# A hybrid encoder layer on one core: gate rows spread by broadcast loads in place of selector matmuls

## The chip, the cores and the metric

The kernel runs on one core of a Trainium2 chip. The metric is the device time of one launch in microseconds. Five engines work side by side, each through its own instructions in order: TensorE (PE, with PEld for the loading of its stationary operand), VectorE (DVE), ScalarE (ACT), GpSimd (POOL) and SyncE (SP), which here only issues DMA transfers. They wait for each other by semaphores.

## The reference

One pre-norm layer on 256 tokens of width 2048, in float32: RMSNorm, one wide input projection, an mLSTM branch and an RG-LRU branch, both in both directions, a sigmoid-gated merge, an output projection, a residual and a last RMSNorm. What the change touches is the weights of the mLSTM branch, with 4 heads and 2 directions:

```python
d_log = jnp.where(lower, bc[..., :, None] - bc[..., None, :] + ic[..., None, :], -jnp.inf)
inter_log = bc + m_st[..., None]
m_row = jnp.maximum(inter_log, jnp.max(d_log, axis=-1))
w_intra = jnp.exp(d_log - m_row[..., None])
scores = jnp.einsum('bhjk,bhsk->bhjs', qc, kc) * w_intra
...
h = num / jnp.maximum(jnp.abs(den), jnp.exp(-m_row))[..., None]
```

Here `bc` is the running sum of the log of the forget gate and `ic` the input gate. The weight of key position s for query position j is an exponential of something that depends on j alone (the row maximum, one number for each partition) plus something that depends on s alone (`ic - bc`, one row of 256 numbers for each head and direction, eight rows in all). The kernel puts the queries on the partitions, so a row over s has to be present in every partition.

## The kernel before, in words

**Products.** Weights arrive as 512 KB chunks of 128 x 1024 float32 numbers. Each product of float32 operands is made from three single-pass products of a high part and a low part: `load_chunk` loads a chunk into one of five `raw` tiles (line 215, SP), ScalarE rounds it into `whi` (line 225), VectorE subtracts to get `wlo` (line 226), and both go into one of four tile pairs. `half_tr` multiplies four such chunks with the transposed input (lines 453 and 456, results `acc`), `pair` makes two blocks of the projection at once with sums and differences of blocks that save products (lines 260 to 263, with extra casts at 266, 319 and 323 and low halves at 267, 320 and 324; its four extra accumulators are the four `aux` tiles). Where a chunk's number in a `pair` is listed in `CASTS`, VectorE makes the high half too (line 223).

**Order.** `tick()` is called at each chunk. It takes one entry from `queue` (the norm, the gates, the mLSTM scores) and one place of each running lane. A lane holds the work of one quarter of the RG-LRU branch and of one mLSTM head; `PLAN` has one row for each of the four lanes, and each string of a row is one place: `c` the convolutions (lines 839 to 844), `g` the gates (858 to 876), `e` and `r` exponentials and roots on ScalarE, `s` the scans (892 to 899), `h` the sum of both directions (904), `m` the product of scores and values (1003 to 1010), `f` its transposition into the next operand (1018 to 1025), `y` sums of blocks of the input for `pair`. `drain()`, once in the first quarter, empties what is left of the queue. The framework then sets the order on each engine by priorities and readiness; weight chunks carry a high priority.

**Gates.** `g_proj`, `g_nat` and `g_cum` make the gates and their running sums. `g_rows` transposes them on TensorE, so that the eight rows stand in partitions 0 to 3 (forward) and 32 to 35 (backward) of `ar` (line 703), and takes running maxima (704, 705). It splits `ar` into a high part (706, ScalarE) and a low part (707, VectorE). `g_max` brings the maxima back onto the partitions (712 to 716). `g_wts(h)` makes, for head h and both directions, the weights: two matmuls with a selector, a 128 x 128 matrix with one row of ones, copy one row of `ar` into all partitions of an `aux` tile in PSUM (722 and 723, high and low part); VectorE adds the negative maximum and a mask (731), ScalarE takes the exponential (733). `s_mul(h)` multiplies queries with keys (772) and weighs them (780 to 793), `s_tr(h)` transposes the result (802), which is split into the tile `sPT` (473 and 474). Four more names: line 466 and 468 fold two halves of a result, 411 to 419 make one block sum (`y`), 758 and 827 scale by the norm.

Of the kernel before, what the change touches and what calls it, by code (L numbers as in the profile page):

```python
# [9 lines left out]
F32 = mybir.dt.float32  # L10
F32R = mybir.dt.float32r
# [4 lines left out]
P = 128  # L16
S = 256
D = 2048
KT = D // P
NB = 512  # L20
KC = 2
HP = 10000000
NH = 4
# [14 lines left out]
SWAP = True  # L38
RAWS = 5
H_FORMS = (4, 0)  # L40
CASTS = {("o", 0): (5,), ("o", 1): (5,), ("o", 2): (5,), ("o", 3): (6,), ("v", 0): (0,), ("v", 2): (2,)}
PT_FORMS = (2, 6)
LATE = {(st, p): (k[p], l[p]) for st, k, l in (("wb", S_WB, L_WB), ("gb", S_GB, L_GB), ("ga", S_GA, L_GA), ("wa", S_WA, L_WA))
        for p in range(2)}
LATE["wo", 0] = (S_WO, L_WO)
HEADS = {("v", 0): (S_V[0], 4), ("o", 0): (S_OZ[0], 12), ("o", 1): (S_OZ[1], 24), ("v", 2): (S_V[1], 36),
         ("o", 2): (S_OZ[2], 44), ("o", 3): (S_OZ[3], 56)}
PLAN = (('y0', '', '', 'c0', '', 'c3', 'y1 c1 g0', '', 'c2 g1', '', '', '', '', 'g2', '', 'g3', '', '', '', '', 'e0 e1', '', '', '', '', 'r1', 'r0 s0', '', 'm0', 'm1 f0', '', 'f1', '', 's1', '', 'h',),
# [3 lines left out]

PK_NORM, PK_HEAD, PK_CB, PK_CW, PK_BRG, PK_LAM = 0, 1, 2, 3, 7, 11
# [3 lines left out]
def f(ap):  # L57
    return ap.bitcast(F32)
# [3 lines left out]
def hybrid_encoder(ctx: ExitStack, tc: tile.TileContext, x, xt, pk, bif, fg, wg, wi, wr, wa, wb, wo, wq, wh, out):  # L62
    nc = tc.nc
    pe, act, dve, pool, sp = nc.tensor, nc.scalar, nc.vector, nc.gpsimd, nc.sync
# [4 lines left out]
    hp = ctx.enter_context(tc.tile_pool(name="hp", bufs=1))  # L69
# [5 lines left out]
    def name(n):  # L75
        uid[0] += 1
        return f"{n}_{uid[0]}"

    def ct(shape, n, dt=F32):
        return cst.tile(shape, dt, tag=n, name=n)  # L80

    def sl(tag, dt=F32, cols=4096):
        return slot.tile([P, cols], dt, tag=tag, name=name("s" + tag))
# [3 lines left out]
    def aux(i=None):  # L87
        if i is None:
            i = auxn[0] % 4
            auxn[0] += 1  # L90
        return paux.tile([P, NB], F32, tag=f"aux{i}", name=name("aux"))
# [17 lines left out]
    queue, lanes = [], []  # L109
# [119 lines left out]
    def block_nat(src, xhi, xlo):  # L229
        ps, _ = acc_pair()  # L230
        for kq in range(KT // KC):
            tick()
            advance()
            hi, lo = load_chunk(src[kq])
            for kk in range(KC):
                k = kq * KC + kk
                wh, wl = hi[:, kk * NB:(kk + 1) * NB], lo[:, kk * NB:(kk + 1) * NB]
                for tb in range(2):
                    o = k * S + tb * P
                    a, b = xhi(o, o + P), xlo(o, o + P)  # L240
                    pe.matmul(ps[tb], a, wh, start=(k == 0), stop=False)
                    pe.matmul(ps[tb], a, wl, start=False, stop=False)
                    pe.matmul(ps[tb], b, wh, start=False, stop=(k == KT - 1))
        return ps
# [254 lines left out]
    def x_raw(k):  # L499
        return xs[:, k * S:(k + 1) * S] if k else x0[:, KT:]  # L500
# [42 lines left out]
    def et(shape):  # L543
        n = int(np.prod(shape[1:]))
        o = eoff[0]
        eoff[0] += n
        v = est[:shape[0], o:o + n]
        if len(shape) == 3:
            v = v.rearrange("p (a b) -> p a b", b=shape[2])
        return v  # L550

    ident = ct([P, P], "ident")
# [24 lines left out]
                       pattern=[[1, P]], channel_multiplier=-1)  # L577

    rt = hp.tile([P, 2 * NB], F32R, tag="vhi", name="rt")
    st_ = hp.tile([P, 2 * NB], F32R, tag="vlo", name="st_")  # L580
    wgp = rt[:, :KT * 32].rearrange("p (k c) -> p k c", c=32)
    selr = st_.rearrange("p (a b) -> p a b", b=P)
    arh, arl = rt[:, 512:768], rt[:, 768:1024]
    for half in range(2):
        pool.tensor_copy(selr[:, half * 4:(half + 1) * 4, :],
                         ident[:, 32 * half:32 * half + 4].rearrange("p (a o) -> p a o", o=1).broadcast_to([P, 4, P]))
    gT, ar, mr = et([P, S]), et([P, S]), et([P, S])
    for t in (gT, mr):
        pool.memset(t, 0.0)
    gn = ct([P, 2, 16], "gn")  # L590
    NS = 48
    cat, ab, ey, sv, qv, pv, ng, spl = (et([P, NS]) for _ in range(8))
    c8, c4 = ct([P, 32], "c8"), ct([P, 32], "c4")
    an = et([P, 2, P])
    negM, em = ct([P, 2, 8], "negM"), ct([P, 2, 8], "em")
# [4 lines left out]
    def wtv(dh, tb):  # L600
        if not wt_:
            wt_.append(sl("A"))
        return wt_[0][:, (dh * 2 + tb) * S:(dh * 2 + tb + 1) * S]
# [27 lines left out]
    def x_scale(i):  # L631
        if i == 0:
            hn.append(sl("B"))
        for k in range(4 * i, 4 * i + 4):
            r = slice(k * S, (k + 1) * S)
            dve.scalar_tensor_tensor(out=hn[0][:, r], in0=x_raw(k), scalar=ng_[:, k:k + 1], in1=rbc,
                                     op0=ALU.mult, op1=ALU.mult)
# [61 lines left out]
    def g_rows():  # L699
        aps = aux()  # L700
        for tb in range(2):
            pe.transpose(aps[:, tb * P:(tb + 1) * P], an[:, tb, :], ident)
        dve.tensor_copy(ar, aps[:, :S])
        dve.tensor_tensor_scan(mr[0:32, :], ar[0:32, :], ar[0:32, :], 0.0, op0=ALU.max, op1=ALU.max)
        dve.tensor_tensor_scan(mr[32:64, ::-1], ar[32:64, ::-1], ar[32:64, ::-1], 0.0, op0=ALU.max, op1=ALU.max)
        act.copy(arh, ar)
        dve.tensor_sub(arl, ar, f(arh))

    def g_max():
        mps = aux()  # L710
# [4 lines left out]
        dve.tensor_add(em, negM, gst["cum"])  # L715
        act.activation(em, em, AF.Exp)

    def g_wts(h):
        for dh in (h, 4 + h):
            d = dh // 4  # L720
            ps = aux()
            pe.matmul(ps[:, :S], selr[:, dh, :], arh, start=True, stop=False)
            pe.matmul(ps[:, :S], selr[:, dh, :], arl, start=False, stop=True)
            for tb in range(2):
                a, b = RECT[(d, tb)]
                if d == 0:
                    mask = mf[:, P:] if tb == 0 else mf
                else:
                    mask = mb if tb == 0 else mb[:, :P]
                w = wtv(dh, tb)[:, a:b]  # L730
                dve.scalar_tensor_tensor(out=w, in0=ps[:, a:b], scalar=negM[:, tb, dh:dh + 1], in1=mask,
                                         op0=ALU.add, op1=ALU.add)
                act.activation(w, w, AF.Exp)

    queue += [lambda: r_load(0), None, lambda: r_load(1), None, lambda: r_load(2), None, lambda: r_load(3), r_sum,
              None, r_row, g_proj, lambda: x_scale(0), g_nat, lambda: x_scale(1), lambda: x_scale(2),
              lambda: x_scale(3), g_cum, g_rows, None, g_max]
    queue += [lambda h=h: g_wts(h) for h in range(NH)]

    ptt = sl("PT", F32R)  # L740
    pthi, ptlo = ptt[:, :NH * 2 * S], ptt[:, NH * 2 * S:]
# [75 lines left out]
    def rg_block(j):  # L817
# [95 lines left out]
        lane = [[] for _ in range(64)]  # L913
        for i, names in enumerate(PLAN[j]):
            lane[i] += [lambda n=n, w=work: w[n]() for n in names.split()]
# [47 lines left out]
    n = 0  # L963
    for (st, h), ((kqs, places), first) in HEADS.items():
        hsrc, d = {}, {}
# [3 lines left out]
        for place, kq in sorted(zip(places, kqs)):  # L969
            if (st, h, kq) not in H_SKIP:  # L970
                hplan.append((first + place, hsrc[kq], d, kq))
        heads[st, h] = dict(hsrc=hsrc, hstaged=d, t2_="zz" if st == "o" and h % 2 == 0 else "vlo",
                             casts=CASTS.get((st, h), ()))

# [118 lines left out]
    late, n = {}, 0  # L1093
# [88 lines left out]
    ps = block_nat(wo[2], mh, ml)  # L1182
# [21 lines left out]
    for tb, a, b, col in ((0, 0, NB, 3), (1, 0, S, 3), (1, S, NB, 4)):  # L1204
        ps = aux()[:, :b - a]
        for k in range(KT):
# [3 lines left out]
            o = k * S + tb * P  # L1210
# [8 lines left out]
        v = y[:, tb * D + 3 * NB + a:(tb + 1) * D]  # L1219
        dve.tensor_mul(v, v, fgs[:, 3 * NB + a:])  # L1220
        for i, (a, b) in enumerate(((0, S), (NB, 2 * NB), (S, NB), (2 * NB, 3 * NB), (3 * NB, D))):
            v = y[:, tb * D + a:tb * D + b]
# [77 lines left out]
```

## Time and profile before

| | |
|---|---|
| median of 3 runs | 1006.82 us (1006.7 to 1006.89) |
| the profiled execution | 1006.64 us |
| its span, first to last instruction | 1004.9 us |
| busy: TensorE / VectorE / ScalarE / GpSimd | 995.2 / 884.7 / 646.1 / 54.8 us |
| lines 722 and 723 | 16 matmuls of 128 x 256, between 86.3 and 99.2 us of the span |
| transfers | 227.39 MB, mean 226 GB/s |

A row of the profile names the line, the engine, the operation and the tiles (what it writes, then what it reads), the shape, a count, the busy time and the mean of one. In a timeline the first number is the start in us from the span's beginning, the second the length of the row; a bracket at its end is the time for which the engine idled just before, and what ended it. Matmuls overlap, so their starts tell more than their lengths.

### The profile page before, as it was taken

Reading aid. Unit: us, or ns where it says so; the run is one execution under the profiler, and the core shown is the slowest. Engines: PE = TensorE matmul, PEld = TensorE weight load, DVE = VectorE, ACT = ScalarE, POOL = GpSimd, SP = SyncE. Lnnn points to the kernel's source line nnn. Section 1 sums busy time; section 2 is a strip of 40 time slices with the busy share of each in tenths; the row PEclk is TensorE's granted clock in tenths of the full one; section 3 lists DMA queues with packets and bytes.
Section 4 is the critical chain, followed back from the end, with each engine's and each line's share of the span. In section 5 each row is a group of like instructions: output and inputs, shape, how many; then the busy total and the mean of one; then the engine's idle time right before and its main releaser. Section 6 shows DMA issues by size and latency. Waiting matters only on the chain.

```text
span 1004.9 us, 13760 instructions
## 1 busy us (share of the span) xinstructions
PE 995.2 (99%) x4945; PEld 842.7 (84%) x4945; DVE 884.7 (88%) x1185; ACT 646.1 (64%) x855; POOL 54.8 (5%) x83
## 2 busy tenths in 40 slices
PE   9999999999999999999999999999999999999996
PEld 8888988888888888888888888888888888888886
DVE  6788899889899988998697799998998998999985
ACT  7646467866886777667965565655666566464662
POOL 1000000001001000100000001010110010100000
PEclk9999999999999999999999999999999999999999
DMA  9665757668578694778457468889889888888662
GB/s 347 249 210 168 217 181 218 221 190 246 173 206 251 214 279 153 259 207 285 148 187 225 155 208 251 262 232 279 255 241 269 266 261 241 243 298 278 193 202 84
DMA packets 65173, 227.39 MB, mean 226 GB/s; under 512 B 7248, under 2 KB 8272, under 8 KB 64720
## 3 DMA queue, kind: packets, MB, share of 16 engines
q1 hardware_dynamic: 57760, 201.07, 58.2%
q0 software_dynamic: 6624, 24.12, 14.0%
q10 hardware_dynamic: 720, 1.31, 0.4%
q8 instruction: 39, 0.64, 0.3%
q14 instruction: 30, 0.25, 0.1%
HBM read 224.38 MB, written 2.10 MB: 225 GB/s over the span
## 4 chain that ended last, share of the span: by engine, by line
PE 97%; DVE 1%; DMA 1%; issue 0%; ACT 0%; SPq 0%; DVEq 0%; ACTq 0%
PE acc L262 16%; PE acc L263 16%; PE acc L260 16%; PE acc L453 15%; PE acc L456 8%; PE aux L262 4%; PE aux L260 4%; PE aux L263 4%; PE acc L435 1%; PE aux L1003 1%; PE aux L859 1%; PE aux L860 1%; PE aux L858 1%; PE aux L1213 1%; PE aux L1214 1%; PE aux L1212 1%
## 5 line engine op out<-in xcount | busy, mean ns | idle before, releaser
L226 DVE TENSOR_TENSOR wlo<-raw,whi 128x1024 fp32r<-128x1024 f32 (+1 forms) x261 | 312.6, 1210 | 45.3 <-ACT whi L225 43.5
L225 ACT CAST whi<-raw 128x1024 fp32r<-128x1024 f32 (+1 forms) x255 | 262.5, 1040 | 136.3 <-PE acc L263 48.1
L262 PE MATMUL acc<-wlo,sHL 128*128 128x512 f32 x494 | 193.0, 391 | 0.3 <-DVE wlo L226 0.3
L263 PE MATMUL acc<-whi,sHL 128*128 128x512 f32 x494 | 192.5, 390 | 0.0
L260 PE MATMUL acc<-whi,sHL 128*128 128x512 f32 x494 | 190.6, 390 | 0.0
L453 PE MATMUL acc<-sHL,whi 128*128 128x512 f32 x704 | 175.8, 393 | 0.0
L453 PEld LDWEIGHTS acc<-sHL,whi 128*128 128x128 f32 x704 | 127.6, 189 | 23.6
L262 PEld LDWEIGHTS acc<-wlo,sHL 128*128 128x128 f32 x494 | 92.8, 188 | 20.2 <-DVE wlo L226 1.3
L323 ACT CAST whi<-t 128x1024 fp32r<-128x1024 f32 x49 | 51.5, 1051 | 88.8 <-DVE t L314 70.8
L263 PEld LDWEIGHTS acc<-whi,sHL 128*128 128x128 f32 x494 | 92.8, 188 | 18.6
L260 PEld LDWEIGHTS acc<-whi,sHL 128*128 128x128 f32 x494 | 92.6, 188 | 18.8
L456 PEld LDWEIGHTS acc<-sHL,wlo 128*128 128x128 f32 x704 | 95.1, 190 | 5.9
L456 PE MATMUL acc<-sHL,wlo 128*128 128x256 f32 x704 | 98.6, 283 | 0.0
L324 DVE TENSOR_TENSOR wlo<-t,whi 128x1024 fp32r<-128x1024 f32 x49 | 60.0, 1224 | 21.8 <-ACT whi L323 21.5
L266 ACT CAST whi<-sum 128x1024 fp32r<-128x1024 f32 x46 | 48.3, 1049 | 27.4 <-PE acc L263 17.1
L267 DVE TENSOR_TENSOR wlo<-sum,whi 128x1024 fp32r<-128x1024 f32 x46 | 56.2, 1222 | 7.1 <-ACT whi L266 7.0
L320 DVE TENSOR_TENSOR wlo<-raw,whi 128x1024 fp32r<-128x1024 f32 x49 | 59.9, 1223 | 2.4 <-ACT whi L319 2.2
L319 ACT CAST whi<-raw 128x1024 fp32r<-128x1024 f32 x49 | 51.5, 1051 | 16.1 <-PE acc L263 9.8
L174 POOL DMA_DIRECT2D sum<-wq x31 | 26.7, 860 | 422.6 <-DVE b L173 164.1
L314 DVE TENSOR_TENSOR t<-raw,t 128x512 f32<-128x512 f32 x49 | 33.8, 689 | 0.2
L192 POOL DMA_DIRECT2D sum<-wh x15 | 13.2, 879 | 375.3 <-DMA sum<-wh 174.5
L262 PE MATMUL acc<-wlo,sA 128*128 128x512 f32 x86 | 33.6, 391 | 0.0
(362 smaller groups left out, 1758.9 us busy)
## 6 DMA issues: line engine op xcount, KB each, us to landing
raw<-wi SPq DMA_DIRECT2D x191, 512.0 KB, 4.6
raw<-wq SPq DMA_DIRECT2D x37, 512.0 KB, 6.2
sum<-wq SPq DMA_DIRECT2D x31, 512.0 KB, 5.6
sum<-wq POOLq DMA_DIRECT2D x31, 512.0 KB, 7.5
raw<-wo SPq DMA_DIRECT2D x24, 512.0 KB, 4.4
raw<-wb SPq DMA_DIRECT2D x18, 512.0 KB, 4.5
raw<-wa SPq DMA_DIRECT2D x18, 512.0 KB, 5.2
sum<-wh SPq DMA_DIRECT2D x15, 512.0 KB, 5.6
```

The lines of the kernel that those rows point to most:

```text
L225: last_copy[0] = act.copy(hi[:, r], raw[:, r]).ins
L226: last_sub[0] = dve.tensor_sub(lo[:, r], raw[:, r], f(hi[:, r])).ins
L260: pe.matmul(ps, a, wh, start=id(ps) not in began, stop=False)
L262: pe.matmul(ps, a, wl, start=False, stop=False)
L263: pe.matmul(ps, b, wh, start=False, stop=stop)
L267: dve.tensor_sub(lo, v, f(hi))
L319: last_copy[0] = act.copy(h3, r2).ins
L320: last_sub[0] = dve.tensor_sub(l3, r2, f(h3)).ins
L323: last_copy[0] = act.copy(four(h2), t2).ins
L324: last_sub[0] = dve.tensor_sub(four(l2), t2, f(four(h2))).ins
L453: pe.matmul(ps[m], hi[:, o:o + P], hl_t[:, 2 * k * S:2 * (k + 1) * S], start=(k == 0), stop=(turn and k == KT - 1), skip_group_check=True)
L456: pe.matmul(ps[m][:, :S], lo[:, o:o + P], hhi(k * S, (k + 1) * S), start=False, stop=(not turn and k == KT - 1), skip_group_check=True)
```

## The change

The eight rows go to a small tile in device memory, `rowd`, by two transfers of 4 x 256 numbers, one for each direction. Two loads (`g_spread(0)` for heads 0 and 1, `g_spread(1)` for heads 2 and 3) read four rows each, 4 KB, and write them into all 128 partitions of the SBUF tile `rows`; both use the same tile, so the second waits until the weights of heads 0 and 1 are made. Line 731 then reads `rows` in place of PSUM. The sixteen matmuls, the selectors (two GpSimd copies) and the split of `ar` go. The queue gets three more entries between `g_max` and the scores: the two loads and two empty places, less one. VectorE no longer makes the first high half of the first `pair` (`("v", 0): (0,)` leaves `CASTS`). In `PLAN`, the first lane starts its convolutions, gates, exponentials, roots and first scan one place earlier, its products `m` stay, its second scan and `h` come one earlier; in the second lane the first `f` comes two places later, in the third the last `f` two places later.

```diff
-CASTS = {("o", 0): (5,), ("o", 1): (5,), ("o", 2): (5,), ("o", 3): (6,), ("v", 0): (0,), ("v", 2): (2,)}
+CASTS = {("o", 0): (5,), ("o", 1): (5,), ("o", 2): (5,), ("o", 3): (6,), ("v", 2): (2,)}
...
-PLAN = (('y0', '', '', 'c0', '', 'c3', 'y1 c1 g0', '', 'c2 g1', '', '', '', '', 'g2', '', 'g3', '', '', '', '', 'e0 e1', '', '', '', '', 'r1', 'r0 s0', '', 'm0', 'm1 f0', '', 'f1', '', 's1', '', 'h',),
+PLAN = (('y0', '', 'c0', '', 'c3', 'y1 c1 g0', '', 'c2 g1', '', '', '', '', 'g2', '', 'g3', '', '', '', '', 'e0 e1', '', '', '', '', 'r1', 'r0 s0', '', '', 'm0', 'm1 f0', '', 'f1', 's1', '', 'h',),
...
-    st_ = hp.tile([P, 2 * NB], F32R, tag="vlo", name="st_")
     wgp = rt[:, :KT * 32].rearrange("p (k c) -> p k c", c=32)
-    selr = st_.rearrange("p (a b) -> p a b", b=P)
-    arh, arl = rt[:, 512:768], rt[:, 768:1024]
-    for half in range(2):
-        pool.tensor_copy(selr[:, half * 4:(half + 1) * 4, :],
-                         ident[:, 32 * half:32 * half + 4].rearrange("p (a o) -> p a o", o=1).broadcast_to([P, 4, P]))
...
+    rows = et([P, 4, S])
+    dram = ctx.enter_context(tc.tile_pool(name="dram", bufs=1, space=bass.MemoryType.DRAM))
+    rowd = dram.tile([8, S], F32, name="rowd")
...
         dve.tensor_copy(ar, aps[:, :S])
+        for d in range(2):
+            sp.dma_start(rowd.rearrange("(r d) s -> r d s", d=2)[:, d, :], ar[d * 32:d * 32 + 4, :])
...
-        act.copy(arh, ar)
-        dve.tensor_sub(arl, ar, f(arh))
...
+    def g_spread(i):
+        src = rowd[4 * i:4 * i + 4, :].rearrange("r s -> (r s)").rearrange("(o n) -> o n", o=1)
+        sp.dma_start(rows.rearrange("p r s -> p (r s)"), src.broadcast_to([P, 4 * S]))
+
     def g_wts(h):
         for dh in (h, 4 + h):
             d = dh // 4
-            ps = aux()
-            pe.matmul(ps[:, :S], selr[:, dh, :], arh, start=True, stop=False)
-            pe.matmul(ps[:, :S], selr[:, dh, :], arl, start=False, stop=True)
+            row = rows[:, 2 * (h % 2) + d, :]
...
-                dve.scalar_tensor_tensor(out=w, in0=ps[:, a:b], scalar=negM[:, tb, dh:dh + 1], in1=mask,
+                dve.scalar_tensor_tensor(out=w, in0=row[:, a:b], scalar=negM[:, tb, dh:dh + 1], in1=mask,
...
-              lambda: x_scale(3), g_cum, g_rows, None, g_max]
-    queue += [lambda h=h: g_wts(h) for h in range(NH)]
+              lambda: x_scale(3), g_cum, g_rows, None, g_max, lambda: g_spread(0)]
+    queue += [None, lambda: g_wts(0), lambda: g_wts(1), lambda: g_spread(1), None, lambda: g_wts(2), lambda: g_wts(3)]
```

In the orders below the changed kernel's lines from 655 on are one to three lower than before (line 709 is 712 before, 702 and 717 are new, 891 is 892, 986 is 987, 1009 is 1010).

TensorE, around the gate weights, before (lines 453 and 456 are products with weight chunks):

```order
L456 MATMUL acc_902<-sHL_90,wlo_977 128x256 x6
L722 MATMUL aux_823<-rt,st__168 128x256
L722 MATMUL aux_831<-rt,st__168 128x256
L722 MATMUL aux_860<-rt,st__168 128x256
L456 MATMUL acc_902<-sHL_90,wlo_977 128x256 x2
L456 MATMUL acc_902<-sHL_90,wlo_999 128x256
L712 MATMUL aux_795<-ident,sE_141 128x128 x2
L723 MATMUL aux_823<-rt,st__168 128x256
```

and in the changed kernel:

```order
L456 MATMUL acc_874<-sHL_90,wlo_939 128x256 x8
L456 MATMUL acc_874<-sHL_90,wlo_961 128x256 x4
L709 MATMUL aux_795<-ident,sE_141 128x128 x2
L456 MATMUL acc_874<-sHL_90,wlo_961 128x256 x4
L453 MATMUL acc_874<-sHL_90,whi_960 128x512 x8
```

The products stand side by side where selectors stood between them; sixteen rows are gone from here and the next 13 us.

SP's queue at the same place, before (all loads of weight chunks):

```order
L215 DMA raw_1186<-wi 128x1024
L215 DMA raw_1215<-wi 128x1024
L215 DMA raw_1237<-wi 128x1024
L215 DMA raw_1259<-wi 128x1024
L215 DMA raw_1312<-wi 128x1024
```

and in the changed kernel, the same loads (1131, 1179, 1201, 1223, 1257) with the writes of the rows (702) and the two loads of them (717; `sE_141` is the tile in which `rows` lies):

```order
L215 DMA raw_1131<-wi 128x1024
L702 DMA rowd<-sE_141 4x256 x2
L215 DMA raw_1179<-wi 128x1024
L717 DMA sE_141<-rowd 128x1024
L215 DMA raw_1201<-wi 128x1024
L215 DMA raw_1223<-wi 128x1024
L717 DMA sE_141<-rowd 128x1024
L215 DMA raw_1257<-wi 128x1024
```

The fourth and the sixth of these wait, the one for the writes to land, the other for VectorE to be done with the first rows, and the loads behind them wait with them.

VectorE at the end of the first lane, before (`sD` of line 892 is the second scan's factor, `zz` of 987 the head's gate, 1010 the head's result):

```order
L396 TENSOR_TENSOR zz_2137<-zz_2137,acc_1906 128x1024
L226 TENSOR_TENSOR wlo_2374<-raw_2372,whi_2373 128x1024
L419 TENSOR_TENSOR sPT_178<-sE_1448,sPT_178 128x512
L987 TENSOR_TENSOR zz_2137<-zz_2137,to_2136 128x1024
L414 TENSOR_TENSOR sE_1448<-sE_1448 128x128
L416 TENSOR_TENSOR sE_1448<-sE_1448 128x128
L226 TENSOR_TENSOR wlo_2410<-raw_2408,whi_2409 128x1024
L892 SCALAR_TENSOR_TENSOR sD_403_1863<-sC_401_1861,sD_403_1863 128x1024
L415 TENSOR_TENSOR sE_1448<-sE_1448 128x128
L1010 SCALAR_TENSOR_TENSOR to_2136<-aux_2266,sq_2264,zz_2137 128x512
```

and in the changed kernel:

```order
L396 TENSOR_TENSOR zz_2115<-zz_2115,acc_1884 128x1024
L419 TENSOR_TENSOR sPT_178<-sE_1426,sPT_178 128x512
L226 TENSOR_TENSOR wlo_2352<-raw_2350,whi_2351 128x1024
L891 SCALAR_TENSOR_TENSOR sD_386_1816<-sC_384_1814,sD_386_1816 128x1024
L414 TENSOR_TENSOR sE_1426<-sE_1426 128x128
L416 TENSOR_TENSOR sE_1426<-sE_1426 128x128
L986 TENSOR_TENSOR zz_2115<-zz_2115,to_2114 128x1024
L226 TENSOR_TENSOR wlo_2394<-raw_2392,whi_2393 128x1024
L892 TENSOR_TENSOR sD_386_1816<-sD_386_1816,sC_385_1815 128x1024
L415 TENSOR_TENSOR sE_1426<-sE_1426 128x128
L226 TENSOR_TENSOR wlo_2416<-raw_2414,whi_2415 128x1024
L1009 SCALAR_TENSOR_TENSOR to_2114<-aux_2244,sq_2242,zz_2115 128x512
```

The scan's first product (892 before, 891 now) has moved ahead of the head's gate, and its second (893 before, 892 now) ahead of the head's result.

4 rows, old and new, of the table PLAN are left out of this document.

## The prediction, as put on record

> **What bounds the kernel now.** I read the page first, then the waits of TensorE, then the timelines of the stretches that the change touches. From the page, the span, two engine rows and the chain that ended last:
>
> ```profile
> span 1004.9 us, 13760 instructions
> ...
> PE 995.2 (99%) x4945; PEld 842.7 (84%) x4945; DVE 884.7 (88%) x1185; ACT 646.1 (64%) x855; POOL 54.8 (5%) x83
> ...
> PE 97%; DVE 1%; DMA 1%; issue 0%; ACT 0%; SPq 0%; DVEq 0%; ACTq 0%
> ```
>
> TensorE works 99% of the span and holds 97% of the chain. Its waits, in order of their sum, first two rows:
>
> ```profile
> PE aux L483 <- DVE wu L518: 1.1, 1, 1.1
> PE acc L262 <- DVE wlo L226: 0.3, 1, 0.3
> ```
>
> One wait at the start and one of 0.3 us in the middle. So time is TensorE's own work plus a few late starts: work taken off TensorE is gained, unless it arrives somewhere earlier than VectorE (88% busy) has its operands ready. VectorE makes the low half of every weight chunk (line 226).
>
> **The sixteen matmuls.** Groups of TensorE, then three neighbouring rows of its timeline:
>
> ```profile
> L723 PE MATMUL aux<-rt,st__168 128*128 128x256 f32 x8 | 2.0, 293 | 0.0
> L722 PE MATMUL aux<-rt,st__168 128*128 128x256 f32 x8 | 1.9, 283 | 0.0
> ```
>
> ```profile
> 93.51 0.28 PE L723 MATMUL aux<-rt,st__168 128*128 128x256 f32 x1
> 93.63 0.28 PE L456 MATMUL acc<-sHL,wlo 128*128 128x256 f32 x1
> 93.75 0.28 PE L722 MATMUL aux<-rt,st__168 128*128 128x256 f32 x1
> ```
>
> One is shown as 283 ns long, but the starts are 0.12 us apart: the rest is pipeline depth that the next one covers. What leaves the path is 16 x 0.12 = 1.92 us, not 16 x 0.283 = 4.5 us. The Trainium skill ("TensorE: Matmul & The Clock Gate", Back-to-back issue gap) gives N/2.4 + 2.5 ns for the gap at the warm clock, which is an estimate of 109 ns for 256 columns and 1.75 us for sixteen; the trace has 120 ns, and decides.
>
> **The two loads and their queue.** The selectors' place is taken by two small writes of the rows to device memory and two loads of 512 KB that copy four rows into all partitions, all on SP's queue, between weight loads. The nearest rows, from the DMA issues (size, median us to landing):
>
> ```profile
> raw<-wi SPq DMA_DIRECT2D x191, 512.0 KB, 4.6
> ...
> sB<-x SPq DMA_DIRECT2D x4, 512.0 KB, 7.7
> ...
> out<-sA SPq DMA_DIRECT2D x4, 128.0 KB, 2.3
> ...
> bifs<-bif SPq DMA_DIRECT2D x1, 0.1 KB, 6.6
> ```
>
> A write to device memory took 2.3 us on a quiet queue; a tiny transfer behind others took 6.6; 512 KB take 4.6, 7.7 in the crowded opening. When the rows are there and when VectorE uses them, from VectorE's timeline and its groups by form:
>
> ```profile
> 81.66 0.42 DVE L703 COPY sE<-aux 128x256 f32<-128x256 f32 x1
> ...
> 87.27 1.23 DVE L226 TENSOR_TENSOR wlo<-raw,whi 128x1024 fp32r<-128x1024 f32 x1 [0.83 <-PE acc L456]
> ...
> 88.70 2.04 DVE L731 SCALAR_TENSOR_TENSOR sA<-aux,negM,sE 128x128 f32<-128x128 f32 x6
> ...
> 99.38 0.74 DVE L731 SCALAR_TENSOR_TENSOR sA<-aux,negM,sE 128x256 f32<-128x256 f32 x2
> ```
>
> ```profile
> L731 DVE SCALAR_TENSOR_TENSOR sA<-aux,negM,sE 128x256 f32<-128x256 f32 x8 | 3.7, 478 | 0.0
> ...
> L731 DVE SCALAR_TENSOR_TENSOR sA<-aux,negM,sE 128x128 f32<-128x128 f32 x8 | 2.5, 344 | 0.0
> ```
>
> The rows stand at 82.1. The writes go out at 82.5 and land between 84.8 (2.3) and 89.1 (6.6); a weight load is ahead of them in the queue, so I take 86.2. First load plus 4.6: 90.8. Eight of the sixteen weight operations, half of 3.7 + 2.5, are 3.1 us: 93.9. The second load, which may not overwrite its rows before, lands at 98.5, and the last eight end at 101.6. Before, the last ended at 99.38 + 0.74 = 100.1. So VectorE's queue is held at line 731 (behind it stand folds, low halves and the next products) and the gate weights are 1.5 us late (bounds: 2 early to 10.6 late, with 6.6 and twice 7.7). Taking the source from SBUF instead of PSUM I cost at nothing.
>
> What covers it: the low half made at 87.27 to 88.50 is used by TensorE (the order's tile numbers pair them) at
>
> ```profile
> 98.72 0.28 PE L456 MATMUL acc<-sHL,wlo 128*128 128x256 f32 x1
> ```
>
> 10.2 us later, so chunks are that far ahead and neither a held SP queue nor a held VectorE shows on TensorE at once. What counts is whether VectorE has caught up when its dense stretch begins. The stretches, each row with its length, the busy time of PE, PEld, DVE, ACT and POOL, the granted clock, the DMA share and GB/s:
>
> ```profile
> 100.00:110.00 10.00, 10.00 (x65) 9.06 (x64) 9.16 (x36) 3.64 (x7) 0.00 (x0) 1.00 0.50 168
> 110.00:120.00 10.00, 10.00 (x67) 9.01 (x66) 7.36 (x9) 4.70 (x7) 1.04 (x1) 1.00 0.93 277
> 120.00:130.00 10.00, 10.00 (x62) 9.00 (x61) 9.97 (x30) 5.88 (x7) 0.87 (x1) 1.00 0.75 207
> ...
> 140.00:150.00 10.00, 10.00 (x52) 8.44 (x51) 10.00 (x19) 5.83 (x8) 0.00 (x0) 1.00 0.62 207
> ```
>
> VectorE is busy 9.16 and 7.36 of 10 us: 0.84 + 2.64 = 3.5 us idle take up the 1.5. Cost: 0. The 1 MB more on the DMA (168 to 277 GB/s in these rows) and the ScalarE copy and subtraction that go are hidden the same way, on both sides: 0.
>
> **The dense stretch, 120 to 163.** Here VectorE does not rest, and chunks come ever closer to their use:
>
> ```profile
> 154.91 0.43 DVE L844 TENSOR_TENSOR sD<-sD,sD 128x256 fp32r<-128x256 f32 x1 [0.40 <-ACT sD L843]
> 155.87 1.23 DVE L324 TENSOR_TENSOR wlo<-t,whi 128x1024 fp32r<-128x1024 f32 x1 [0.53 <-ACT whi L323]
> ...
> 160.28 0.69 DVE L314 TENSOR_TENSOR t<-raw,t 128x512 f32<-128x512 f32 x1
> 160.88 1.23 DVE L226 TENSOR_TENSOR wlo<-raw,whi 128x1024 fp32r<-128x1024 f32 x1
> ```
>
> ```profile
> 163.24 0.39 PE L262 MATMUL acc<-wlo,sHL 128*128 128x512 f32 x1
> ```
>
> The low half ends at 162.11 and TensorE wants it at 163.24: 1.13 us to spare. In the changed order three 512-wide matmuls (0.23 us each) stand behind this point that stood before it, so beside the 1.92, which moves VectorE's start of the stretch (a fold of TensorE's result) just as far, TensorE comes 0.68 sooner. VectorE, from that fold to this chunk, has in the new order two line 474, one 411, one 419 and one 417 more, and one 223 (the dropped cast) and one 314 less: with 0.60 from start to start for a 128x512 (the rows at 160.28 and 160.88) and 0.2 for 417, +0.6 x 4 + 0.2 - 0.6 x 2 = +1.4. So 1.13 - 0.68 - 1.4 = -0.95, if none of the 0.40 + 0.53 that VectorE idles above is filled by that work, and about 0 if all is. The term is a new stall between 0 and 0.95; most of the idling waited for ScalarE, whose gate sigmoids now come a lane place earlier, so I take 0.3. The cast that moves from VectorE to ScalarE is about 1 us on an engine at 5.9 of 10: 0.
>
> **A late start that may go, at 252.** TensorE, then VectorE:
>
> ```profile
> 251.74 0.46 PE L858 MATMUL aux<-sD,whi 128*128 128x256 f32 x2
> 252.51 0.50 PE L262 MATMUL acc<-wlo,sHL 128*128 128x512 f32 x1 [0.32 <-DVE wlo L226]
> ```
>
> ```profile
> 228.88 1.23 DVE L987 TENSOR_TENSOR zz<-zz,to 128x1024 f32<-128x1024 f32 x1 [1.06 <-ACT zz L986]
> ...
> 233.50 0.75 DVE L1010 SCALAR_TENSOR_TENSOR to<-aux,sq,zz 128x512 f32<-128x512 f32 x1 [0.52 <-POOL sq L1009]
> ```
>
> Two 256-wide matmuls from 251.74 would free TensorE at 251.98; it starts at 252.51, 0.53 late, for a low half on which VectorE was behind. With the scan one place earlier, its first product (line 892, 1.1 us) stands in the changed order ahead of line 987, in the 1.06 that idles there, and the second (893) ahead of 1010 with its 0.52. Up to 1.5 us of the backlog goes, 0.53 is needed: -0.53 (0 if the root is not ready for it).
>
> **Another at 462.**
>
> ```profile
> 461.44 0.40 PE L260 MATMUL acc<-whi,sHL 128*128 128x512 f32 x1
> 461.95 0.50 PE L260 MATMUL acc<-whi,sPT 128*128 128x512 f32 x1
> ```
>
> ```profile
> 447.60 0.69 DVE L313 TENSOR_TENSOR t<-sum,raw 128x512 f32<-128x512 f32 x1 [0.45 <-DMA raw<-wh]
> ```
>
> 0.51 between starts in place of 0.23: 0.28 late. One tap of the convolution (line 841) moves in the new order from behind line 313 into the 0.45 idle before it. Between -0.28 and 0; I take -0.2. The second lane's edit (`f0` later) leaves VectorE's order there as it was: 0.
>
> **Sum.** -1.92 + 0.3 - 0.53 - 0.2 = -2.35. The profiled execution took 1006.64 (span 1004.9 and 1.7 around it), 0.18 below the median of 1006.82; the difference is taken off the median: **1004.5**, by the skill's gap 1004.6.
>
> **Rivals.**
> (a) The gain is eaten in the dense stretch. For it: VectorE at 9.97 and 10.00 of 10 there, and +1.4 of work; against: 0.93 of idling inside. With the full 0.95 and both late starts staying: -1.92 + 0.95 = -0.97, **1005.8**.
> (b) Only the matmuls go; what is won and lost elsewhere is nil: **1004.9**.
> (c) Slower: the rows come late and VectorE's queue waits for them. Write 6.6 and loads of 7.7: the last weights end at 89.1 + 7.7 + 3.1 + 7.7 + 3.1 = 110.7, 10.6 late; 3.5 are idle time, 7.1 go into the dense stretch, which has 1.13 to spare: a stall of 6.0, less 1.92, **1010.9**. It decides from 3.5 + 1.13 + 1.92 = 6.6 us of lateness. Against it: the queue is far less crowded at 85 than in the opening, where 6.6 and 7.7 were seen.
> Beside (c) stands the Trainium skill ("DMA: Bandwidth & Descriptors", Rules for kernel authors): a load that reads what a DMA wrote must wait for its completion, as SP does here. Its Anatomy section puts about 2 us on each transfer before the bytes at 436 GB/s: an estimate of 2 + 3.2 us, rows at 87.7, before VectorE asks for them, and no hold. The 2.3 us write agrees, the 4.6 us load does not.
>
> **Chances.** Forecast 0.50, (a) 0.27, (b) 0.15, (c) 0.08. The range from 1003.6 (all gains in full, no new stall, 1003.8 and a little) to 1006.5 holds the first three and leaves (c) out. About 0.2%, 2.0 us, is what a measurement of this kernel tells from no change. Faster than that, under 1004.8: most of the forecast (0.43), a third of (b) and a little of (a): 0.53. Slower: (c), 0.08. The same: 0.39.
>
> **What would show it.** Right: no rows of lines 722 and 723; TensorE still at 99% with some 993 us busy; line 262 after 251 without a wait; a hold at the weight operations near 89 to 91 on VectorE that is gone by 117. Wrong: new TensorE waits on low halves between 150 and 175 of more than 1 us together (then (a)), or a landing of either load later than 8 us after its issue (then (c)). The forecast also fails if the changed order brings a stall after 270, where I count on none.

## The result, and the profile after

The changed kernel takes 1004.47 us (median of 8 runs, 1003.63 to 1005.16), the kernel before beside it 1007.37 (8 runs, 1006.7 to 1008.12): a ratio of 0.9971, 95% interval 0.996 to 0.9981. The forecast was 1004.5, with a range of 1003.6 to 1006.5 that holds it. It was counted from a kernel before of 1006.82, and what it forecast was a gain of 2.35; the gain measured side by side is 2.9 here and 2.5 in a second set. The experiments below show that the number was better than its reasons.

The page of the changed kernel, its span, the engines and the chain that ended last; then the only two waits of TensorE that it lists:

```profile
span 1003.3 us, 13726 instructions
...
PE 993.9 (99%) x4929; PEld 841.2 (84%) x4929; DVE 883.6 (88%) x1183; ACT 646.3 (64%) x855; POOL 55.0 (5%) x81
...
PE 96%; DVE 2%; issue 1%; DMA 1%; ACT 0%; DVEq 0%
```

```profile
PE aux L483 <- DVE wu L518: 1.1, 1, 1.1
PE acc L262 <- DVE wlo L226: 0.8, 1, 0.8
```

Sixteen matmuls fewer, TensorE still 99% busy. But the wait for a low half, 0.3 us in all before, is now 0.8. It isn't the one at 252. TensorE and VectorE of the changed kernel:

```profile
250.81 0.50 PE L262 MATMUL acc<-wlo,sHL 128*128 128x512 f32 x1
...
447.56 0.39 PE L260 MATMUL aux<-b,sHL 128*128 128x512 f32 x1
448.79 0.50 PE L262 MATMUL acc<-wlo,sHL 128*128 128x512 f32 x1 [0.84 <-DVE wlo L226]
```

```profile
446.91 0.69 DVE L313 TENSOR_TENSOR t<-sum,raw 128x512 f32<-128x512 f32 x1 [1.23 <-DMA raw<-wh]
```

A 512-wide matmul follows the last after 0.23 us; this one after 1.23, so it is 1.00 late. VectorE, which makes its low half, had stood 1.23 us for a weight load. In the kernel before, VectorE waited for that same load too, 0.45 us, and TensorE was not touched.

The rows that were to come late, on SP's queue and on VectorE (line numbers here are one lower than before):

```profile
82.29 0.62 SPq L702 DMA_DIRECT2D rowd<-sE  x2
...
84.89 0.34 SPq L717 DMA_DIRECT2D sE<-rowd  x1
...
93.28 0.33 SPq L717 DMA_DIRECT2D sE<-rowd  x1
```

```profile
90.53 2.72 DVE L730 SCALAR_TENSOR_TENSOR sA<-sE,negM 128x128 f32<-128x128 f32 x8 [1.82 <-DMA sE<-rowd]
...
99.90 0.34 DVE L730 SCALAR_TENSOR_TENSOR sA<-sE,negM 128x128 f32<-128x128 f32 x1
```

The last weight operation ends at 100.24, where it ended at 100.1 before.

For the comparison of many kernels I add up TensorE's late starts: the time from one start to the next less the usual one for that width (0.227, 0.120 and 0.109 us for 512, 256 and 128 columns), where it is over 0.1. "TensorE" in the table is the time from one and the same matmul (line 453, at 44 us; the opening ahead of it differs by up to 1 us between executions) to TensorE's last end, "end" what the span has behind that. The columns between are sums of late starts in three stretches, us. Each row of these is one profiled execution; time and ratio are of all runs. The profiled execution of the kernel before (1006.64) was shorter than all eight of its runs in the first row, that of the changed kernel (1005.16) the longest of its eight, so these two profiles alone show less of the gain than the medians.

| kernel | time (runs) | ratio to before, 95% | TensorE | 100-200 | 240-275 | 440-475 | end |
|---|---|---|---|---|---|---|---|
| before | 1007.37 (8) | | 953.0 | 0 | 0.65 | 0.39 | 7.9 |
| changed | 1004.47 (8) | 0.9971 (0.996-0.9981) | 951.8 | 0.11 | 0.37 | 1.11 | 7.4 |
| changed, once more | 1004.86 (9) | 0.9976 (0.9966-0.9985) | 951.0 | 0.11 | 0.38 | 0.32 | 7.4 |
| loads alone | 1006.58 (11) | 0.9993 (0.9984-1.0002) | 953.5 | 1.02 | 0.64 | 1.87 | 8.2 |
| loads alone, once more | 1007.25 (11) | 0.9998 (0.9989-1.0007) | 953.6 | 1.01 | 0.64 | 1.90 | 8.2 |
| tables alone | 1005.22 (11) | 0.9978 (0.997-0.9987) | 951.9 | 0 | 0 | 0 | 7.2 |
| changed, first row back | 1004.85 (11) | 0.9978 (0.9969-0.9987) | 952.6 | 0.33 | 1.74 | 0.39 | 7.4 |
| changed, third row back | 1005.35 (11) | 0.9978 (0.9969-0.9987) | 952.1 | 0.11 | 0.37 | 1.43 | 7.4 |
| changed, cast back | 1004.47 (11) | 0.9978 (0.9969-0.9986) | 950.4 | 0.27 | 0 | 0 | 8.2 |
| changed, two loads exchanged | 1005.72 (11) | 0.9987 (0.9979-0.9996) | 950.5 | 0.11 | 0.37 | 0 | 7.4 |
| the same, once more | 1005.21 (9) | 0.9979 (0.9969-0.9989) | 950.6 | 0.11 | 0.36 | 0 | 7.4 |
| second load twice | 1005.28 (11) | 0.9983 (0.9974-0.9992) | 952.7 | 1.62 | 0.36 | 0.53 | 7.4 |
| both loads twice | 1007.09 (11) | 1.0002 (0.9993-1.0011) | 954.0 | 3.49 | 0.37 | 0 | 7.3 |
| before, selectors five times | 1015.35 (4) | 1.0087 (1.0073-1.0101) | 961.3 | 0 | 0.85 | 0.88 | 7.9 |

The kernel before ran again beside each set: 1007.33, 1006.86 and 1007.07. So kernels of different sets are compared by the ratio, not by the time.

### The profile page after: what moved, and what is told of

Read it like the earlier page. It is cut to its first block, busy times and chain, and to the rows that moved or that the text cites. A ratio compares the mean times of both kernels' runs of the same rounds, so it can differ in the third digit from the quotient of the medians.

```text
span 1003.3 us, 13726 instructions
## 1 busy us (share of the span) xinstructions
PE 993.9 (99%) x4929; PEld 841.2 (84%) x4929; DVE 883.6 (88%) x1183; ACT 646.3 (64%) x855; POOL 55.0 (5%) x81
## 4 chain that ended last, share of the span: by engine, by line
PE 96%; DVE 2%; issue 1%; DMA 1%; ACT 0%; DVEq 0%
PE acc L262 16%; PE acc L263 16%; PE acc L260 16%; PE acc L453 15%; PE acc L456 8%; PE aux L262 4%; PE aux L263 4%; PE aux L260 4%; PE acc L435 2%; PE aux L1002 1%; PE aux L858 1%; PE aux L859 1%; PE acc L438 1%; PE aux L857 1%; PE aux L1213 1%; PE aux L1212 1%
## 5 line engine op out<-in xcount | busy, mean ns | idle before, releaser
L313 DVE TENSOR_TENSOR t<-sum,raw 128x512 f32<-128x512 f32 x46 | 31.5, 685 | 4.3 <-DMA sum<-wq 2.7
```

## The experiments

**The two halves apart.** Loads alone: the changed code with the old `CASTS` and `PLAN`. Tables alone: the old code with the new ones.

```diff
 # loads alone, against the changed kernel
-CASTS = {... ("o", 3): (6,), ("v", 2): (2,)}
+CASTS = {... ("o", 3): (6,), ("v", 0): (0,), ("v", 2): (2,)}
 # and PLAN's first three rows as before; tables alone: the other way round
```

> The two writes, the two broadcast loads and the missing selectors, with the tables of lane places and casts of the kernel before. Theory of the prediction: the 1.92 us of the sixteen matmuls go and nothing else changes, so 1.9 us below the kernel before; the late starts of TensorE at about 250 (0.53) and 460 (0.28) stay. Rival 1 (a later collision eats it: in the changed kernel TensorE waits 1.0 us at 448.8, where a weight chunk that VectorE sums, line 313, comes from a DMA that did not come as much earlier as TensorE did): the same 1.0 us wait shows here too, and the time is 0.9 to 1.2 us below. Rival 2 (VectorE sets the time downstream, so that less work on TensorE only makes its late starts longer): the late start at 250 grows from 0.53 to 1.5 or more, and the time is less than 0.7 us below.

> The sixteen selector matmuls as before, with the new tables of lane places and casts. Theory of the prediction: +0.3 in the dense stretch, -0.53 at 252, -0.2 at 462, so 0.4 us below the kernel before. By the trace of the changed kernel: -0.3 at 252, -0.3 at 462, +0.1 at 161, so 0.5 us below if the wait at 448.8 comes from TensorE being early (it is not early here), and 0.5 us above if that wait of 1.0 us comes from the third lane's new order.

> The changed kernel once more, for the comparison on this chip: 2.3 to 2.9 us below the kernel before. Its profile tells whether the wait of 1.0 us at 448.8 comes in every execution (then it belongs to the order) or only in some (then the DMA of that moment sets it, and a profiled execution without it is 0.7 to 1.1 us shorter in its span).

> The loads with all the old tables once more. If the late starts of TensorE at 151.3 (0.31) and 161.3 (0.48), 252.1 (0.53) and 461.9 to 462.9 (0.28 and 0.38) belong to the order of the instructions, they are here again within 0.1; the wait at 450.4 (0.88), if the DMA of the moment sets it, comes out anywhere from 0 to 1. The time 0.4 to 1.2 below the kernel before.

The theory of the prediction falls here. The loads alone, with the sixteen matmuls gone, are 0.75 us below the kernel before in one set and 0.18 above in the other, and both intervals hold 1. The tables alone are 2.1 below, with all sixteen matmuls. The loads' 1.92 did leave TensorE, and it came back as late starts, the same ones in both profiles to within 0.04: 1.0 between 150 and 162, 0.9 with 0.11 behind it at 450, and 0.5 more than before at 462. Both profiles are of longer executions, 1007.77 and 1007.49; 8 of the 22 runs took 1005.7 to 1006.1, and no profile shows which of these late starts they lack. TensorE, ScalarE and VectorE of loads alone, second profile:

```profile
150.93 0.50 PE L260 MATMUL aux<-sB,sHL 128*128 128x512 f32 x1
...
160.28 0.49 PE L260 MATMUL acc<-whi,sHL 128*128 128x512 f32 x1
160.99 0.50 PE L260 MATMUL aux<-whi,sF 128*128 128x512 f32 x1 [0.22 <-ACT sC L861]
...
450.14 0.50 PE L262 MATMUL acc<-wlo,sHL 128*128 128x512 f32 x1 [0.76 <-DVE wlo L226]
```

```profile
146.95 1.05 ACT L266 CAST whi<-sum 128x1024 fp32r<-128x1024 f32 x1 [1.94 <-PE acc L263]
148.02 1.28 ACT L861 ACT_TABLE_LOAD   x1
149.31 1.57 ACT L861 ACTIVATE sC<-aux,pks 128x256 f32<-128x256 f32 x4
```

```profile
448.26 0.69 DVE L313 TENSOR_TENSOR t<-sum,raw 128x512 f32<-128x512 f32 x1 [1.98 <-DMA raw<-wh]
```

At 150.9 TensorE wants an `aux` tile that the gate sigmoids (861) read until 150.88; a table load of 1.28 and a cast stand ahead of them. With the new tables the same sigmoids stand ahead of the cast, and are over by 148.3:

```profile
145.42 1.28 ACT L861 ACT_TABLE_LOAD   x1
146.71 1.57 ACT L861 ACTIVATE sC<-aux,pks 128x256 f32<-128x256 f32 x4
...
148.96 1.06 ACT L266 CAST whi<-sum 128x1024 fp32r<-128x1024 f32 x1
```

In the kernel before the sigmoids were later still (152.23 to 153.80), but the order put the matmul that wants their tile at 155.87. That 861 holds up the matmul at 150.9 is read from these times; the profile names it only for the one at 161. The order of each engine is made when the kernel is built: it came out anew between 80 and 185 us, not only shorter by sixteen, and I had read the loads' part as if the rest of the order stood still. Which part of the edit made it anew is not separated: the queue of loads alone also has four more entries, not three as said further up (two loads and two empty places).

From 185 us on the orders of TensorE, VectorE and ScalarE are those of the kernel before, operation by operation. So the late start at 450 and the larger of the two at 462, which are new, came without any new order there. Both hang on one load: it took 6.1 us in both profiles, 4.6 in the kernel before, and landed at 448.4 and 448.2, where it landed at 447.5 before. At 450 VectorE's 1.98 above shows it; at 462 the way is longer. VectorE works without a rest from the 448.26 above to 460.4, and the casts of ScalarE for the matmul at 462 wait for the end of that:

```profile
460.55 1.05 ACT L323 CAST whi<-t 128x1024 fp32r<-128x1024 f32 x1 [3.46 <-DVE t L314]
```

**Which table does what.**

```diff
 # third row back
-..., 'f0', 'h', '', 'f1',),
+..., 'f0', 'f1 h',),
 # first row back: the whole first row as before; cast back: ("v", 0): (0,) in CASTS again
```

> The changed kernel with the third lane's row of the table put back. If the wait of 1.0 us at 448.8 comes from that row's new order, it is gone, the late start at 462 (0.28) is back, and the time is 0.7 us below the changed kernel, about 3.2 us below the kernel before. If it comes from TensorE being 1.8 us early against a DMA that is not, the wait stays (0.8 to 1.2 us) and the time is 0 to 0.3 us above the changed kernel, 2.2 to 2.6 below the kernel before.

> The changed kernel with the first lane's row of the table put back (loads, cast and the other rows as changed). With the loads and all the old tables TensorE was late at 151.3 (0.31) and 161.3 (0.48) for gate products of ScalarE (line 861) and at 252.1 (0.53) for a low half of VectorE. Theory: the first lane's row, which starts the gates one place earlier and the scan one place earlier, is what takes these away; then all three are back here, 0.2 to 0.4 more with the starts behind them, and the time is 0.9 to 1.4 us above the changed kernel. Rival: the moved cast does it by freeing VectorE; then they stay away and the time is within 0.3 of the changed kernel.

> The changed kernel with the one cast (line 223, 0.69 us a piece) back on VectorE. Prediction: the cast was costed at nothing for ScalarE, and its going freed 0.6 us on VectorE in the dense stretch, where the changed kernel has 0.5 us to spare at 161; so a late start of 0.1 to 0.6 us between 130 and 163, and the time 0.1 to 0.6 above the changed kernel. Rival: the cast carries the gain of the tables; then TensorE is late there by 0.8 or more.

The third row takes away the late starts at 461 (0.27, 0.39 and 0.11 behind each are back without it) and not the wait at 449, which stays in all kernels that come early there with the old queue, except with the cast back. With the loads in, the first row takes away most of what stands at 250: without it 1.74, with it 0.37. It doesn't by itself account for the gates at 151 and 161: these return only where row and cast are both old, and with them the second and third rows (0.33 and 0.27 of late starts with one of them old, 1.0 with all). So I had the dense stretch half right. At 252 the row does help, but the rest goes when the cast is back on VectorE, which no part of the forecast has. In time neither row can be told from the changed kernel (ratio 0.9978 for both). With the cast back TensorE's part is the shortest of all, 950.4, and yet the time is that of the changed kernel: what TensorE wins, the end of the program loses (8.2 in place of 7.4, last section). That it has no wait at 449 is not the cast's own doing: from 262 us on its orders are those of the changed kernel, and the load took 4.6 us in that execution. No run moves the cast alone.

**The load at 441.** The wait at 449 was 1.00, 0.21, 0.28, 0.44 and 0.42 in the five profiles with the loads and new tables, whole or in part, in which it stands (changed twice, first row back, third row back, second load twice). It went with the time that the load took: 5.7 us, 4.9, 5.0, 5.7 and, by the start of line 313, 5.1. With 4.6 (tables alone, cast back) there was none. The changed kernel's queue, and the one where the two loads are exchanged, the only difference between the orders of the two kernels on any engine:

```diff
-                    with tc.issue_after(last_dma[0]):
+                    with tc.issue_after(hr2[0] if place == 60 else last_dma[0]):
 # hr2[0] is the load of line 285; the partial sum for place 60 is asked for four places later
```

```profile
439.47 0.33 SPq L189 DMA_DIRECT2D sum<-wh  x1
441.06 0.33 SPq L285 DMA_DIRECT2D raw<-wh  x1
```

```profile
441.88 0.33 SPq L285 DMA_DIRECT2D raw<-wh  x1
442.26 0.46 SPq L189 DMA_DIRECT2D sum<-wh  x1
```

> The changed kernel with two loads exchanged in the queue of SP near 440: the 512 KB for the next partial sum, which is not wanted before 454, goes behind the weight load that VectorE waits for at 446.9 (line 313), not ahead of it. If that load is late because the other's bytes share the DMA with it (5.7 us in place of 4.6), it lands up to 1.1 us sooner, the wait of TensorE at 448.8 (0.2 to 1.0 us so far) falls to 0.2 or less, and the time is 0.2 to 0.8 below the changed kernel. If its issue, which waits for a buffer, sets its landing, the wait stays at 0.2 to 1.0. If the sum is then late, a new wait of 0.2 to 1 us stands at 457 to 462.

> The changed kernel with the two loads exchanged near 440 once more. In its first profile the weight load took 3.4 us and TensorE did not wait at 448, yet its times were spread over 1003.8 to 1008.6. If the exchange costs something later in some executions, the profile shows a wait between 455 and 465 when its time is above 1005, and the median is again above 1005; if the spread was of that session, the times lie within 1 us and the median is 0.2 to 0.8 below the changed kernel's 2.5 below the kernel before.

The mechanism is as the first theory had it: the load takes 3.4 us in place of 5.7, VectorE doesn't wait, and TensorE has no late start between 440 and 475 in either profile:

```profile
446.42 0.69 DVE L313 TENSOR_TENSOR t<-sum,raw 128x512 f32<-128x512 f32 x1
```

So the load was late because another 512 KB, wanted later, was issued 1.6 us ahead of it; that the two share the DMA is the likely reason. Why it takes 4.6 us behind that neighbour in one execution and 6.1 in another stays open. The time is another matter: the medians, 1005.72 and 1005.21, aren't below the changed kernel's, and the runs spread over 1003.8 to 1008.6 and 1003.7 to 1006.1. The two executions that were profiled took 1004.70 and 1003.98, so no profile shows what the longer ones wait for. That stays open.

**The price of a selector matmul.**

```diff
+            for _ in range(5):
-            pe.matmul(ps[:, :S], selr[:, dh, :], arh, start=True, stop=False)
+                pe.matmul(ps[:, :S], selr[:, dh, :], arh, start=True, stop=False)
 # and the second product likewise
```

> The kernel before with each selector product made five times over into the same place: 64 matmuls of 256 columns more, the output the same. By the prediction's price, 0.12 from start to start, TensorE is 64 x 0.12 = 7.7 us later at the end; by the Trainium skill's gap of 109 ns 7.0; by the shown length of 0.283 18. Less what VectorE, with that much more time, is no longer late for: 0.53 at 252 and 0.28 at 462, so 6.7 to 7.7 above the kernel before.

```profile
92.08 0.28 PE L723 MATMUL aux<-rt,st__168 128*128 128x256 f32 x1
...
93.28 0.28 PE L723 MATMUL aux<-rt,st__168 128*128 128x256 f32 x1
```

Ten starts in 1.20 us (lines 723 and 724 are 722 and 723 of the kernel before). TensorE is 8.3 longer: 64 x 0.12 = 7.7 and 0.5 more of late starts. The time is 8.5 longer. The price was right, and the shown length (18) does not fit. By the 109 ns of the Trainium skill ("TensorE: Matmul & The Clock Gate", Back-to-back issue gap) it would have been 7.0; the trace has 120. The other half of the expectation was wrong: 7.7 us more for VectorE at 90 did not remove the late starts at 250 and 462; they are 0.85 and 0.88 in place of 0.65 and 0.39. From 118 us on the orders are those of the kernel before, and a shift of everything by 8 us leaves the late starts where they stood in them. The 0.5 more at the second place goes with the load just described: VectorE waited for it 1.00 us here, 0.45 in the kernel before.

**Late rows.** Each broadcast load twice, or the second one only; the second copy waits on SP's queue for the first.

```diff
-        sp.dma_start(rows.rearrange("p r s -> p (r s)"), src.broadcast_to([P, 4 * S]))
+        for _ in range(2):          # second load twice: range(1 + i)
+            sp.dma_start(rows.rearrange("p r s -> p (r s)"), src.broadcast_to([P, 4 * S]))
```

> The changed kernel with each broadcast load issued twice, the second copy behind the landing of the first on SP's queue. First rows then at 95 (90.5 + 4.6), their eight operations end at 98, the second pair lands at 106.5 and the last weight operation ends at 109, 9 us later than the 100.2 of the changed kernel. By the prediction's rule (a held VectorE costs what exceeds its idle time, here 1.25 + 0.51 + 0.26 between 100 and 163, and the 0.5 us to spare at 161) TensorE stalls 6.5 us around 150 to 165, and the time is 6.5 above the changed kernel. Rival: the stall is smaller, under 2, because VectorE works on in other places while TensorE lives on the chunks made 10 us ahead, and has rest again after 163. Second rival: the weight loads held behind the copies on SP's queue come late, and TensorE waits for a high half (ScalarE, line 225) or a low half before 120.

> The changed kernel with only the second broadcast load issued twice: last weight operation at 104.6 in place of 100.2, 4.4 us late. By the same rule 4.4 - 2.0 - 0.5 = 1.9 us of stall around 150 to 165 and 1.9 above the changed kernel; by the rival no stall and no difference beyond 0.4.

VectorE with both twice, then with the second twice:

```profile
94.21 1.14 DVE L731 SCALAR_TENSOR_TENSOR sA<-sE,negM 128x128 f32<-128x128 f32 x3 [3.06 <-DMA sE<-rowd]
...
110.02 2.72 DVE L731 SCALAR_TENSOR_TENSOR sA<-sE,negM 128x128 f32<-128x128 f32 x8 [3.58 <-DMA sE<-rowd]
```

```profile
102.40 2.72 DVE L731 SCALAR_TENSOR_TENSOR sA<-sE,negM 128x128 f32<-128x128 f32 x8 [4.21 <-DMA sE<-rowd]
```

The last weights come at 112.7 and 105.1, 12.5 and 4.9 us late. TensorE is late mostly where the rule said, at 155 to 163, and once earlier: by 0.95 at 136 with both twice, by 0.40 at 115 with the second twice. With both twice:

```profile
136.38 0.47 PE L260 MATMUL acc<-whi,sHL 128*128 128x512 f32 x1 [0.79 <-DVE xp L468]
...
159.12 0.51 PE L262 MATMUL aux<-wlo,sF 128*128 128x512 f32 x1 [1.14 <-DVE wlo L324]
```

But it is late by 3.4 and 1.5 more than in the changed kernel, where the rule gives 12.5 - 2.5 = 10 and 2.4. VectorE's row of the stretch 80 to 170 (columns as in the prediction), changed kernel, both twice, second twice:

```profile
80.00:170.00 90.00, 90.00 (x501) 78.19 (x500) 84.62 (x173) 57.59 (x91) 3.42 (x4) 1.00 0.66 210
```

```profile
80.00:170.00 90.00, 87.87 (x486) 75.33 (x485) 80.02 (x166) 55.32 (x87) 2.76 (x3) 1.00 0.67 208
```

```profile
80.00:170.00 90.00, 89.19 (x494) 76.92 (x493) 82.75 (x172) 57.03 (x89) 2.77 (x3) 1.00 0.69 211
```

VectorE did 4.6 and 1.9 us less than in the changed kernel. The stalls of 3.4 and 1.5 follow that, not the lateness: with both twice other work (folds, low halves) was ordered ahead of the weights, so much of the lateness was not lost. That the lost work is the cause is argued from these two runs; the 1.2 and 0.4 between are not measured on their own, and some of the loss is VectorE waiting for a late TensorE. The time with both twice equals that of the kernel before; with the second twice it is 0.7 to 1.2 above the changed kernel by the ratios, whose intervals overlap.

## Why the prediction was right, and where it was not

The time was right to 0.1 us, in part by luck: the kernel before ran 0.55 us longer beside the changed one than in the median that the forecast was taken from, and two errors of the sum cancel. One of the prediction's own signs of being wrong, a stall after 270, came. The steps, one by one:

- **Sixteen matmuls, -1.92.** The price (0.12) holds, five times over. That it leaves the path does not hold by itself: alone it won nothing that can be told from zero. With the new tables it wins 0.1 to 0.9 on TensorE (951.9 with the tables alone, 951.8 and 951.0 with both) and 0.4 in time beside each other (1005.22 and 1004.86), which the intervals do not tell from zero. The step that failed is the rule set up at the start, that work taken off TensorE is gained unless it arrives somewhere earlier than VectorE is ready: I looked for such places in the stretches that the diff names, and the two that took the gain when the loads came alone were the gates of ScalarE (1.0 at 151 and 161) and a weight load issued near 441 (1.0 at 450, 0.5 more at 462).
- **Tables, -0.43 in all.** They are worth 2.1 alone. In the profiles 1.1 of it is on TensorE (late starts of 0.65, 0.39 and 0.2 at 326 are gone) and 0.8 in the end of the program. The forecast came out right since this error and the one above cancel.
- **Loads and their queue, 0.** Right. The writes went out at 82.29, as forecast, and were done by 84.89, at most 2.6 us; I took 3.7. The loads took 5.6 (84.89 to 90.5) and 3.6 (93.28 to 96.9) where I took 4.6 for each, and the hold of VectorE at 90.53 stands where I said it would. The estimate from the Trainium skill ("DMA: Bandwidth & Descriptors", Anatomy) was 3.2 us for a load, made for transfers that GpSimd issues, and both of these, issued by SP, took longer; with 2 us for the writes it had the rows there at 87.7 and no hold, where they came at 90.5 and VectorE was held 1.82. The lateness is 0.1 and not 1.5. The lower bound of "2 early" does not come out of its rows: a write of 2.3 and two loads of 4.6 end the weights at 100.2, where they did end. The operation from SBUF costs what it cost from PSUM (0.478 and 0.347 us, before 0.478 and 0.344).
- **Dense stretch, +0.3.** One late start of 0.11 at 161. What made it small was the gates coming earlier, named there as a help; the lane row or the moved cast does it, either alone to 0.3, and only with both old is it 1.0.
- **252, -0.53.** From 0.54 to 0.26, half. Line 891 moved ahead of 986 and its idle time went; 1009 still waits 0.73 for GpSimd, and the 1.5 of idle time was not all filled. In the tables alone and with the cast back it is zero.
- **462, -0.2.** 0.28 became nothing, 0.39 with the start behind it; it returns with the third row put back.
- **A stall after 270, counted as none.** It came: 0.2 to 1.0 at 449, as large as the gains at 252 and 462 together. The profile before had the sign, VectorE's 0.45 for that load at 447.60. I quoted that row as an idle time to be filled, and did not ask what happens when TensorE arrives 1.8 us sooner, VectorE 1.5 and the load only 0.7 (it landed at 446.8, 447.5 before).
- **Rivals.** (a) is what the loads alone do: 1.0 in the dense stretch against the 0.95 worked out. (b), only the matmuls count, is refuted by the tables alone. (c) was priced too high: it decides not at 6.6 us of lateness but at about 12.5, where the time is that of the kernel before.
- **The range.** Its lower end is given as all gains in full, 1003.8 and a little; 1.92, 0.53 and 0.28 off 1006.82 are 1004.1.

None of the versions tried beats the changed kernel by more than these measurements tell.

## What to carry to other kernels

A kernel whose bound engine has no idle time may still give nothing back for work taken off it, if the others are only just in time: run the removal alone before believing its sum, and look for idle times of the second engine on a transfer far behind the edit, since here the load did not come as much earlier as the engines did. Where the order is made at build time, an edit can bring a new order, here for 100 us behind it; late starts that stand in an order were taken away here by changing it (a load exchanged with its neighbour, a lane place), not by more time ahead of them. In two runs here a held queue cost about the work that its engine lost, far less than the lateness of what it waited for.

## What the runs showed of the hardware that I had not expected

**The end of the program has two lengths.** The page's row for a queue that loads instructions, and the last store that ScalarE's queue issues, of the kernel before:

```profile
q14 instruction: 30, 0.25, 0.1%
```

```profile
999.24 0.87 ACTq L1227 DMA_DIRECT2D out<-sA  x2
```

The same two of the changed kernel:

```profile
q14 instruction: 29, 0.24, 0.1%
```

```profile
998.16 0.86 ACTq L1226 DMA_DIRECT2D out<-sA  x2
```

From these stores to the end of the span (1004.9 and 1003.3) it is 5.7 and 5.1 us. All fourteen profiles fall in two groups: 5.7 to 5.9 with 30 packets in that row (the five with the cast on VectorE), and 4.9 to 5.2 with 29 (the nine with it on ScalarE). The last two stores land about 0.8 us later in the first group, and the trace has one 8 KB instruction packet there 5.1 to 5.3 us behind TensorE's end, among the stores; in the second group that packet comes after the span. So a cast moved from one engine to another seems to have been worth 0.5 to 0.8 us by the length of a program, not by its work, a part of the 2.1 of the tables that no term of the forecast has. That the packet delays the stores is argued from these times; no run separates it from the cast.

**A queue neighbour sets a load's time.** The same 512 KB load took 4.6 to 6.1 us in the ten profiles that show its landing behind another 512 KB issued 1.2 to 1.6 us earlier, and 3.4 in the two where it went first.
